# A planner that knows its side tasks' two banks: one layer of a hybrid decoder on one core

## The chip, the cores and the metric

The program runs on one core of one Trainium2 chip. The metric is device microseconds of one execution, the median of several runs. A profiled execution gives the trace that is read below.

## The reference, cut to what matters

One layer over 2048 positions of width 1024. A modulation, one projection, two groups of heads, an output projection with LayerNorm, and a SwiGLU with LayerNorm. The second head group is a recurrence over time:

```python
def rwkv7_scan(r, decay, k, v, a_vec, b_vec):
    def step(state, inp):
        r_t, w_t, k_t, v_t, a_t, b_t = inp
        sa = jnp.einsum('bhvk,bhk->bhv', state, a_t)
        state = (state * w_t[:, :, None, :] + sa[..., None] * b_t[:, :, None, :]
                 + v_t[..., None] * k_t[:, :, None, :])
        return state, jnp.einsum('bhvk,bhk->bhv', state, r_t)
...
        h = x * (1.0 + sc1) + sh1
        p = h @ w_in[l]
        mix = jnp.concatenate([short_conv_mixer(p_conv), rwkv7_mixer(p_shift)], -1) @ w_out[l]
        x = layer_norm(DEEPNORM_ALPHA * x + (1.0 + gt1) * mix, ln1_g[l], ln1_b[l])
        h = x * (1.0 + sc2) + sh2
        gate, up = jnp.split(h @ w_ffn_in[l], 2, axis=-1)
        f = (jax.nn.silu(gate) * up) @ w_ffn_out[l]
        x = layer_norm(DEEPNORM_ALPHA * x + (1.0 + gt2) * f, ln2_g[l], ln2_b[l])
```

## The kernel before, in words

**Two stages.** In the first, some 1,500 us long, the sequence is cut into four quarters of 512 positions. For each quarter TensorE runs the projection as dense products (tiles `d_...`, the output projection's `do_...`; each operand split into a high and a low part, three matmuls of 128x512 per block). The recurrence is cut into chunks of 64 positions; one quarter of one pair of heads is a *unit*, sixteen in all, written `q_hp` (0_0 to 3_3). A unit is a chain of some twenty short TensorE steps with evacuations by ScalarE, VectorE or GpSimd between them. The second stage is the SwiGLU as a fast matrix scheme (tiles `f`, then `o`).

**TensorE's order is written out by a planner.** `Interleave` holds one main stream (the dense products, `MM` = 0.216 planner-us each) and a list of side tasks (`unit`, `add`, `norm`, `mod_sums`), all Python generators. A side task yields (cost, wait[, condition]): it comes again when the planner's clock has passed the wait and the condition holds. When no side task is due, one dense matmul is put out. Only TensorE's order is fixed so; the other engines' instructions are ordered by a scheduler, except where `behind(...)` holds one behind all that its engine has been given.

**A unit's steps**, by the names that rows show: `z`, `a`, `ss`, `v`, `b` (preparation), `sn` (whose result is `Np`), `at`, `sk`, `bt`, `sr` (two banks), `x`; then the solve of the chunk's triangular system: `Np` goes out to memory and comes back as `Ns`, VectorE makes fifteen pairs of a product `pr` and a sum `G`, and `G` returns through memory in another layout (`Gd`, then eight transfers into `H16`, shown as `H`). ScalarE copies `H16` into `Gf`, VectorE transposes it to `LT`, and `pz`, `pd`, `pq`, `pg` finish the solve. Then `w` twice, `m`, `ry`, the state chain `s` (eight steps, TensorE and VectorE in turn), the output `y`, and the tail: mean and variance, `yc`, `pt` (a transpose), `yo`, `g` (the gate) and `yg`. Between the solve's last `G` and `pz` the planner leaves `D_GH` and 1.5.

**Banks.** `mm` (3) belongs to the dense products. The side tasks' steps share the tag `rb` with two banks (`RBB`); `mtt` and `ht` of `add` and `norm` are in it too. `sv` (one bank) holds `pz`, `pd`, `pq`, `pg` and also the tail's `pt` and `g`; `ch` and `y` hold the state chain and the output. A TensorE step on a bank that is still being read stops TensorE, since its order is fixed.

**The output projections** of quarters 0 to 2 are parts of the main stream (`ORDER`); that of quarter 2 stops after its first two tiles until `norm` of quarter 1 is done, and only side tasks run meanwhile.

Of the kernel before, what the change touches and what calls it, by code (L numbers as in the profile page):

```python
# [49 lines left out]
D_SS, D_B, D_SC, D_EV, D_W, D_CH, D_PT, D_G = 2.09, 7.34, 4.73, 1.5, 2.2, 1.3, 12.0, 3.34  # L50
D_ST, D_NS, D_TR, D_GH = 1.1, 13.0, 2.0, 11.0
MM = 0.216
# [18 lines left out]
class Interleave:  # L71
# [4 lines left out]
    def __init__(self):  # L76
        self.now, self.tasks = 0.0, []

# [16 lines left out]
    def __call__(self, stream, last=True):  # L95

        more = True
        while more or any(last or not t[3] for t in self.tasks):
            if self.side():
                continue  # L100
            cost = next(stream, 0) if more else None
            if cost == 0:
                more = False
            elif cost is not None:
                self.now += cost
            elif self.tasks and not self.side():
                self.now = min(t[0] for t in self.tasks if t[0] > self.now)


@with_exitstack  # L110
def kernel(
# [183 lines left out]
    def out_proj(q, spawn, raws=None):  # L295
# [12 lines left out]
        def add(n, mt):  # L308
            yield 0, 1.2
            pst = psum.tile([P, 4, P], F32, tag="rb", bufs=RBB, name=f"mtt{q}_{n}")  # L310
            for a in range(4):
                pe.transpose(pst[:, a, :], mt[:, a * P:(a + 1) * P], ident)
            xs = xz[:, :, n * P:(n + 1) * P]
            dve.scalar_tensor_tensor(out=xs, in0=xs, scalar=ALPHA, in1=pst, op0=ALU.mult, op1=ALU.add)
            yield 0.45, 0

        def norm():
            yield 0, 3.0
            for a in range(4):
                z = xz[:, a, :]  # L320
                rs = norm_stats(z, f"a{q}_{a}")
                act.activation(z, z, AF.Identity, scale=rs[:, 0:1], bias=rs[:, 1:2])
                t0 = q * QT + a * P
                load(out=xhd[t0:t0 + P, :], in_=z)
            yield 0, D_N
            hb = lnp.tile([P, KT, P], F32, tag="hb", name=f"hb{q}", bufs=1)
            for a in range(4):
                z = xz[:, a, :]
                t0 = q * QT + a * P
                for n in range(2):  # L330
                    ps = psum.tile([P, 4, P], F32, tag="rb", bufs=RBB, name=f"ht{q}_{a}_{n}")
                    for i in range(4):
                        k = 4 * n + i
                        pe.transpose(ps[:, i, :], z[:, k * P:(k + 1) * P], ident)
                    for i in range(4):
                        k = 4 * n + i
                        act.activation(hb[:, k, :], ps[:, i, :], AF.Identity, scale=s2[:, k:k + 1],
                                       bias=b2[:, k:k + 1])
                    load(out=h2d[4 * n:4 * n + 4, :, t0:t0 + P].rearrange("k p t -> p k t"),
                         in_=hb[:, 4 * n:4 * n + 4, :])  # L340
                    yield 0.45, D_H
            done.add(("norm", q))
# [15 lines left out]
    with ExitStack() as ph1:  # L358
# [63 lines left out]
        def unit(n, q, hp, r, kx, vx, lo):  # L422
# [40 lines left out]
            act.activation(sq, kx, AF.Square, scale=k_k[:, hp:hp + 1])  # L463
            yield 1.3, D_SS
            pss = psum.tile([P, NC_Q], F32, tag="rb", bufs=RBB, name="ss" + u)
# [17 lines left out]
            split(rkh, rkl, rk, dve)  # L483
            yield 0, D_B, until("y", n - 2)
            Pc = rw.tile([P, NC_Q, C + 1], F32, tag="Pc", name="Pc" + u, bufs=2)
            pool.memset(Pc[:, :, 0:1], 1.0)
# [20 lines left out]
            done.add(("prep", n))  # L507
            yield 1.5, D_SC


            first = tuple(slice(C * h, C * h + C) for h in range(2))
            ps = rb("sn")
            each(lambda c, h, hr, kr: pe.matmul(ps[hr, c, :], BK[hr, c, first[h]], Ak[hr, c, :], start=True, stop=True))
            Np = rw.tile([P, NC_Q, C], F32, tag="Np", name="Np" + u, bufs=2)
            with behind(dve):
                dve.tensor_tensor(out=Np, in0=ps, in1=rn2.unsqueeze(2).to_broadcast([P, NC_Q, C]), op=ALU.mult)
            yield 1.15, D_ST
            AV = rw.tile([P, NC_Q, 2, C], F32, tag="AV", name="AV" + u, bufs=2)
            ps1 = rb("at")
            each(lambda c, h, hr, kr: pe.matmul(ps1[hr, c, :], Ak[hr, c, :], ident[hr, hr], start=True, stop=True))  # L520
            act.copy(out=AV[:, :, 0, :], in_=ps1)
            yield 1.15, D_ST
            ps2 = rb("sk")
# [6 lines left out]
            BT = []  # L530
            for c4 in range(2):
                t = rw.tile([P, 4, 2 * C], F32, tag="BT", name=f"BT{u}_{c4}", bufs=4)
                ps3 = rb(f"bt{c4}", (4, P))
                for ci in range(4):
                    pe.transpose(ps3[:, ci, :], BK[:, 4 * c4 + ci, :], ident)
                act.copy(out=t, in_=ps3)
                BT.append(t)
                yield 0.45, D_ST

            ps4 = [rb(f"sr{h}") for h in range(2)]  # L540
            each(lambda c, h, hr, kr: pe.matmul(ps4[h][:, c, :], BK[hr, c, :], R[hr, c, :], start=True, stop=True))
# [5 lines left out]
            done.add(("bk", n))  # L547
            yield 1.8, 2 * D_ST
            ps5 = rb("x")
# [81 lines left out]
            for c4 in range(2):  # L631
                cs4 = slice(4 * c4, 4 * c4 + 4)
                ps = rb(f"w{c4}", (4, 2, C))
                for ci in range(4):
# [7 lines left out]
                yield 1.0, D_W if c4 else D_ST  # L642

            ps = rb("m")
            each(lambda c, h, hr, kr: pe.matmul(ps[hr, c, :], WT[hr, c, :], BT[c // 4][hr, c % 4, hr],
                                                start=True, stop=True))
            MT = rw.tile([P, NC_Q, C], F32, tag="MT", name="MT" + u, bufs=1)
            dve.tensor_tensor(out=MT, in0=ps, in1=id64, op=ALU.add)
            yield 1.15, D_ST
            ps1 = rb("ry")  # L650
# [11 lines left out]
            for c in range(NC_Q):  # L662
# [4 lines left out]
                if c == 0:  # L667
# [19 lines left out]
            pool.tensor_tensor(out=vs, in0=vs, in1=nhalf[:, 0:NC_Q], op=ALU.pow)  # L687
            pool.tensor_tensor(out=yc, in0=yc, in1=vs.unsqueeze(2).to_broadcast([P, NC_Q, C]), op=ALU.mult)
            yield 0, D_PT
            psT = psum.tile([P, NC_Q, C], F32, tag="sv", name="pt" + u, bufs=1)  # L690
            each(lambda c, h, hr, kr: pe.matmul(psT[hr, c, :], yc[hr, c, :], ident[hr, hr], start=True, stop=True))
            yo = t2k("yo", "yo" + u)
            act.activation(yo, psT.rearrange("p c t -> p (c t)"), AF.Identity, scale=vecs[:, V_LG + hp:V_LG + hp + 1],
                           bias=vecs[:, V_LB + hp:V_LB + hp + 1])
            pool.tensor_tensor(out=yo, in0=yo, in1=bv, op=ALU.add)
            yield 0.43, D_G
            psG = psum.tile([P, 512], F32, tag="sv", name="g" + u, bufs=1)
            pe.matmul(psG, gu[:, cols], sg, start=True, stop=True)
# [201 lines left out]
        def stream():  # L900

            for q in range(NQ):
# [8 lines left out]
                while todo:  # L911
                    at = 0
                    while todo[at][0] == "u" and not ready(NHP * q + int(todo[at][1])):
                        at = next((j for j, x in enumerate(todo) if x[0] in "co"), None)
                        if at is None:
                            yield None
                            at = 0
# [416 lines left out]
```

## Time and profile before

| | us |
|---|---|
| median of 3 runs (3058.71 to 3065.69) | 3062.82 |
| the profiled execution, its own time | 3061.64 |
| its span in the trace | 3059.8 |
| TensorE busy in the span | 2719.9 (89%) |
| VectorE, GpSimd, ScalarE busy | 1994.5, 1494.7, 1136.5 |
| mean granted clock of TensorE | 0.936 of full speed |

TensorE is busy almost throughout, so what it waits for, and at which clock it runs, is what can change. A granted clock of 1.0 is 2.4 GHz, 0.5 is 1.2 GHz; values between are means over a stretch.

### The profile page before, as it was taken

The page shows a single profiled execution, that of the slowest core. Times are in us where ns is not written, and L with a number is a line of the kernel's source. Part 1 is how long each engine was busy: PE and PEld are TensorE (multiplying, and loading weights), DVE is VectorE, ACT ScalarE, POOL GpSimd, SP SyncE. Part 2 cuts the span into 40 slices and gives each one's busy share as a digit, 9 for nine tenths or more (in the row PEclk, how much of TensorE's full clock was granted, in tenths as well). Part 3 has the DMA queues.
Part 4 walks back from the last instruction along what each step waited for, and adds up shares of the span by engine and source line. Part 5 has one row for each costly group of instructions (what it writes and reads, how often), then busy time and mean ns, then how long its engine had stood idle before and what let it go on. Part 6 is the DMA issues. An engine that isn't in the chain of part 4 may idle for free.

```text
span 3059.8 us, 50282 instructions
## 1 busy us (share of the span) xinstructions
PE 2719.9 (89%) x19232; PEld 2115.6 (69%) x19232; DVE 1994.5 (65%) x3029; ACT 1136.5 (37%) x2072; POOL 1494.7 (49%) x1171
## 2 busy tenths in 40 slices
PE   7878898889999898888779999988999988988986
PEld 5656676666777676666567888866888866766864
DVE  7445555454444645544554777798777787899698
ACT  4543433333533333333454333333333323344333
POOL 4654333323433333333544444456444467578596
PEclk8878999989999999989889999998999999999998
DMA  6442211132521221123553423223232353333333
GB/s 233 133 133 85 81 59 58 57 101 79 161 64 56 82 58 58 58 75 97 163 199 114 144 98 104 100 80 134 100 103 100 104 196 117 106 115 114 101 110 100
DMA packets 223001, 323.72 MB, mean 106 GB/s; under 512 B 55844, under 2 KB 78372, under 8 KB 222760
## 3 DMA queue, kind: packets, MB, share of 16 engines
q1 hardware_dynamic: 222760, 320.50, 33.3%
q8 instruction: 151, 2.47, 0.3%
q14 instruction: 90, 0.74, 0.1%
HBM read 244.39 MB, written 76.03 MB: 105 GB/s over the span
## 4 chain that ended last, share of the span: by engine, by line
PE 59%; DVE 18%; DMA 6%; POOL 6%; issue 4%; ACT 2%; SPq 2%; DVEq 0%; ACTq 0%; POOLq 0%
PE d L260 11%; PE f L227 9%; PE f L228 9%; PE f L226 9%; PE do L260 4%; DVE pr L575 3%; PE o L227 2%; PE o L228 2%; PE o L226 2%; DVE ws L955 2%; POOL ol L223 2%; DMA Gd<-G 2%; SPq L580 1%; DVE fl L223 1%; DMA wm<-in_wmod_dram 1%
## 5 line engine op out<-in xcount | busy, mean ns | idle before, releaser
L223 POOL TENSOR_TENSOR l<-r,h 128x512 fp32r<-128x512 f32 x201 | 266.6, 1328 | 488.3 <-ACT h L222 380.8
L226 PE MATMUL f<-uh,wh 128*128 128x512 f32 x1232 | 494.5, 401 | 10.8 <-ACT wh L222 8.1
L227 PE MATMUL f<-ul,wh 128*128 128x512 f32 x1232 | 493.0, 400 | 8.4 <-POOL ul L223 4.2
L228 PE MATMUL f<-uh,wl 128*128 128x512 f32 x1232 | 492.5, 400 | 4.7 <-POOL wl L223 4.6
L223 POOL TENSOR_TENSOR wl<-ws,wh 128x512 fp32r<-128x512 f32 x220 | 302.9, 1378 | 370.8 <-ACT wh L222 320.6
L955 DVE TENSOR_TENSOR ws<-w,w 128x512 f32<-128x512 f32 x330 | 302.7, 938 | 45.4 <-POOL ol L223 38.5
L227 PE MATMUL o<-ol,fh 128*128 128x512 f32 x616 | 252.3, 413 | 53.4 <-POOL ol L223 53.2
L974 DVE TENSOR_TENSOR c<-f,c 128x512 f32<-128x512 f32 x264 | 181.7, 688 | 159.6 <-PE f L228 95.5
L226 PEld LDWEIGHTS f<-uh,wh 128*128 128x128 f32 x1232 | 234.6, 190 | 70.8 <-ACT wh L222 10.0
L227 PEld LDWEIGHTS f<-ul,wh 128*128 128x128 f32 x1232 | 234.5, 190 | 68.4 <-POOL ul L223 6.6
L228 PEld LDWEIGHTS f<-uh,wl 128*128 128x128 f32 x1232 | 234.5, 190 | 64.5 <-POOL wl L223 7.9
L222 ACT CAST wh<-ws 128x512 fp32r<-128x512 f32 x220 | 136.7, 621 | 360.9 <-DVE ws L955 238.1
L228 PE MATMUL o<-oh,fl 128*128 128x512 f32 x616 | 246.3, 407 | 5.6 <-DVE fl L223 5.3
L226 PE MATMUL o<-oh,fh 128*128 128x512 f32 x616 | 219.8, 404 | 14.1 <-DVE c L974 6.8
L223 POOL TENSOR_TENSOR ol<-ws,oh 128x512 fp32r<-128x512 f32 x110 | 176.9, 1612 | 89.8 <-ACT oh L222 85.5
L222 ACT CAST h<-r 128x512 fp32r<-128x512 f32 x201 | 123.6, 616 | 205.3 <-PE d L260 169.5
L223 DVE TENSOR_TENSOR fl<-fr,fh 128x512 fp32r<-128x512 f32 x154 | 181.0, 1185 | 26.1 <-ACT fh L222 25.3
L227 PEld LDWEIGHTS o<-ol,fh 128*128 128x128 f32 x616 | 121.0, 196 | 96.4 <-POOL ol L223 70.8
L223 POOL TENSOR_TENSOR lo<-ro,ho 128x512 fp32r<-128x512 f32 x64 | 84.9, 1332 | 195.8 <-ACT ho L222 160.0
L226 PEld LDWEIGHTS o<-oh,fh 128*128 128x128 f32 x616 | 118.2, 193 | 45.5 <-ACT oh L222 12.4
L223 POOL TENSOR_TENSOR wl<-w,wh 128x512 fp32r<-128x512 f32 x88 | 118.6, 1348 | 60.7 <-ACT wh L222 60.7
L228 PEld LDWEIGHTS o<-oh,fl 128*128 128x128 f32 x616 | 120.4, 196 | 36.6 <-DVE fl L223 11.7
(501 smaller groups left out, 6021.9 us busy)
## 6 DMA issues: line engine op xcount, KB each, us to landing
r<-in_win_dram SPq DMA_DIRECT2D x201, 256.0 KB
w<-in_wfi_dram SPq DMA_DIRECT2D x176, 256.0 KB
fr<-fd SPq DMA_DIRECT2D x154, 256.0 KB
fd<-fs SPq DMA_DIRECT2D x110, 256.0 KB
wm<-in_wmod_dram SPq DMA_DIRECT2D x72, 256.0 KB
ro<-in_wout_dram SPq DMA_DIRECT2D x64, 256.0 KB
fd<-th SPq DMA_DIRECT2D x44, 256.0 KB
w<-in_wfo_dram SPq DMA_DIRECT2D x44, 256.0 KB
```

The costliest lines, as they stand in the source:

```text
L222: act.copy(out=hi, in_=raw)
L223: (lo_eng or pool).tensor_sub(lo, raw, hi)
L226: pe.matmul(ps, lh, rh, start=start, stop=False)
L227: pe.matmul(ps, lh, rl, start=False, stop=False)
L228: pe.matmul(ps, ll, rh, start=False, stop=stop)
L260: pe.matmul(ps, l[:, ks], r, start=kk == 0 and i == 0, stop=kk == KT - 1 and i == 2)
L575: dve.tensor_tensor(out=v, in0=G[:, :, :t + 1], in1=Nv[:, :t + 1, t].unsqueeze(1).to_broadcast([P, 8, t + 1]), op=ALU.mult)
L580: load(out=H16[16 * b:16 * b + 16, :, b % 4 * 16:b % 4 * 16 + 16], in_=Gd[b].rearrange("c j t -> j c t"))
L955: (eng or dve).tensor_tensor(out=out, in0=blocks[a], in1=blocks[b.lstrip("-")], op=ALU.subtract if b[0] == "-" else ALU.add)
L974: dve.tensor_tensor(out=c[b, t], in0=in0, in1=in1, op=op)
```

## The change

`Interleave` gets a list of the two `rb` banks, each with the planner's time at which it will be free. `run.free(n)` is a condition (n banks are free now), `run.take(n, lag)` occupies n of them until `lag` later (`D_RB` = 3.0 if none is given). Every step that uses `rb` now yields with `run.free()` first and then takes; where a step had a yield before it, the condition is joined to that, elsewhere a yield of cost 0 is added. If nothing is due, the planner's clock also jumps to the next time of a bank. Costs and waits change at `add` (1.2 to 2.0) and before `x` (1.8 and 2.2 to 2.3 and 1.1). `D_GH` goes from 11 to 15. In the tail the multiplication of `yc` and the addition to `yo` go from GpSimd to VectorE, and `pt` and `g` move from the bank `sv` to `y`. In `stream` an output projection can no longer be taken ahead of `f0`.

```diff
-D_ST, D_NS, D_TR, D_GH = 1.1, 13.0, 2.0, 11.0
+D_ST, D_NS, D_TR, D_GH = 1.1, 13.0, 2.0, 15.0
+D_RB = 3.0
...
-        self.now, self.tasks = 0.0, []
+        self.now, self.tasks, self.banks = 0.0, [], [0.0] * RBB
+
+    def free(self, n=1):
+
+        return lambda: sorted(self.banks)[n - 1] <= self.now
+
+    def take(self, n=1, lag=None):
+
+        self.banks = sorted(sorted(self.banks)[n:] + [self.now + (D_RB if lag is None else lag)] * n)
...
-                self.now = min(t[0] for t in self.tasks if t[0] > self.now)
+                self.now = min(t for t in [t[0] for t in self.tasks] + self.banks if t > self.now)
...
-            yield 0, 1.2
+            yield 0, 2.0, run.free()
+            run.take()
             pst = psum.tile([P, 4, P], F32, tag="rb", bufs=RBB, name=f"mtt{q}_{n}")
...
+                    yield 0, 0, run.free()
+                    run.take(1, D_H + 1)
                     ps = psum.tile([P, 4, P], F32, tag="rb", bufs=RBB, name=f"ht{q}_{a}_{n}")
...
-            yield 1.15, D_ST
+            yield 1.15, D_ST, run.free()
+            run.take()
             AV = rw.tile([P, NC_Q, 2, C], F32, tag="AV", name="AV" + u, bufs=2)
             ps1 = rb("at")
...
+            yield 0, 0, run.free(2)
+            run.take(2, 4.5)
             ps4 = [rb(f"sr{h}") for h in range(2)]
...
-            yield 1.8, 2 * D_ST
+            yield 2.3, D_ST, run.free()
+            run.take()
             ps5 = rb("x")
...
-            pool.tensor_tensor(out=yc, in0=yc, in1=vs.unsqueeze(2).to_broadcast([P, NC_Q, C]), op=ALU.mult)
+            dve.tensor_tensor(out=yc, in0=yc, in1=vs.unsqueeze(2).to_broadcast([P, NC_Q, C]), op=ALU.mult)
             yield 0, D_PT
-            psT = psum.tile([P, NC_Q, C], F32, tag="sv", name="pt" + u, bufs=1)
+            psT = psum.tile([P, NC_Q, C], F32, tag="y", name="pt" + u, bufs=1)
...
-            pool.tensor_tensor(out=yo, in0=yo, in1=bv, op=ALU.add)
+            dve.tensor_tensor(out=yo, in0=yo, in1=bv, op=ALU.add)
             yield 0.43, D_G
-            psG = psum.tile([P, 512], F32, tag="sv", name="g" + u, bufs=1)
+            psG = psum.tile([P, 512], F32, tag="y", name="g" + u, bufs=1)
...
-                        at = next((j for j, x in enumerate(todo) if x[0] in "co"), None)
+                        at = next((j for j, x in enumerate(todo) if x[0] in "co" and "f0" not in todo[:j]), None)
```

The same lines with `run.free()` and `run.take()` stand before `ss`, `v`, `sn`, `sk`, `bt`, `w`, `m` and `ry`.

**Three places in the built order.** TensorE where unit 3_1's `pz` comes (the names' first number is the head pair: `pz_1` is unit 3_1, `pt_0` and `g_0` the tail of 3_0, `sn_2` and `at_2` unit 3_2, `d_2` and `d_3` dense tiles of the projection). Before:

```order
L260 MATMUL d_2_12491<-h_4l,h_2_1_12512 128x512
L513 MATMUL sn_2_12521<-Ak_2_12446,BK_2_12339 64x64 x16
L691 MATMUL pt_0_12540<-kst,yc_0_12381 64x64 x16
L592 MATMUL pz_1_12560<-LT_1_12517,Np_1_11819 64x64 x16
L520 MATMUL at_2_12580<-kst,Ak_2_12446 64x64 x16
L260 MATMUL d_2_12491<-h_4h,l_2_1_12513 128x512
L260 MATMUL d_2_12491<-h_5h,h_2_1_12512 128x512
L260 MATMUL d_2_12491<-h_5l,h_2_1_12512 128x512
L599 MATMUL pd_1_12601<-H_136,Z_1_12577 64x64 x16
L698 MATMUL g_0_12624<-sg_10532,gu 128x512
L524 MATMUL sk_2_12629<-Ak_2_12446,BK_2_12339 64x64 x16
```

And in the changed kernel:

```order
L269 MATMUL d_3_12617<-h_1h,h_3_0_12620 128x512
L720 MATMUL pt_0_12628<-kst,yc_0_12473 64x64 x16
L616 MATMUL pz_1_12648<-LT_1_12605,Np_1_11836 64x64 x16
L269 MATMUL d_3_12617<-h_1l,h_3_0_12620 128x512
L269 MATMUL d_3_12617<-h_1h,l_3_0_12621 128x512
L269 MATMUL d_3_12617<-h_2h,h_3_0_12620 128x512
L269 MATMUL d_3_12617<-h_2l,h_3_0_12620 128x512
L269 MATMUL d_3_12617<-h_2h,l_3_0_12621 128x512
L530 MATMUL sn_2_12672<-Ak_2_12571,BK_2_12503 64x64 x16
L727 MATMUL g_0_12691<-sg_10239,gu 128x512
L623 MATMUL pd_1_12696<-H_136,Z_1_12665 64x64 x16
L538 MATMUL at_2_12720<-kst,Ak_2_12571 64x64 x16
```

Before, `pz_1` follows `pt_0` and `sn_2` with no dense product between; now `sn_2` comes after `pz_1`, with five dense products between them, and `g_0` precedes `pd_1`. Counted through the whole order, a unit's `sn` and its `pz` stand 131 to 174 dense products apart before and 158 to 193 now; for each unit the distance grows by 15 to 32, by 24 in the mean.

VectorE in the middle of the same unit's fifteen pairs of `pr` and `G` (`Pi`, `BK`, `rk`, `rn`, `tz`, `x` are preparation of the next unit, `S` steps of the state chain of the unit before). Before:

```order
L473 TENSOR_TENSOR Pi_2_12277<-Pi_2_12277,k_2_12186 128x512
L575 TENSOR_TENSOR pr_1_12056<-G_1_12054,Ns_1_12052 128x56
L469 TENSOR_SCALAR rn_2_12326<-ss_2_12309 128x8
L665 TENSOR_SCALAR Sst_124<-s_0_12126,Pc_0_10971 128x64
L475 TENSOR_TENSOR BK_2_12339<-Pi_2_12277,x_2_12281 128x8x64
L577 TENSOR_REDUCE G_1_12054<-pr_1_12056 128x8
L470 RECIPROCAL rn_2_12326<-rn_2_12326 128x8
L575 TENSOR_TENSOR pr_1_12056<-G_1_12054,Ns_1_12052 128x64
L480 SCALAR_TENSOR_TENSOR rk_2_12342<-rk_2_12342,vecs,r_2_12083 128x512
L577 TENSOR_REDUCE G_1_12054<-pr_1_12056 128x8
L575 TENSOR_TENSOR pr_1_12056<-G_1_12054,Ns_1_12052 128x72
```

Now:

```order
L694 TENSOR_SCALAR S_0_12221<-s_0_12223,Pc_0_10903 128x64
L599 TENSOR_TENSOR pr_1_12127<-G_1_12125,Ns_1_12123 128x64
L601 TENSOR_REDUCE G_1_12125<-pr_1_12127 128x8
L425 SCALAR_TENSOR_TENSOR k_2_12325<-d_18_12249,vecs,A 128x511
L427 SCALAR_TENSOR_TENSOR k_2_12325<-carry,vecs,A 128x1
L599 TENSOR_TENSOR pr_1_12127<-G_1_12125,Ns_1_12123 128x72
L694 TENSOR_SCALAR S_0_12221<-s_0_12223,Pc_0_10903 128x64
L601 TENSOR_REDUCE G_1_12125<-pr_1_12127 128x8
L599 TENSOR_TENSOR pr_1_12127<-G_1_12125,Ns_1_12123 128x80
L601 TENSOR_REDUCE G_1_12125<-pr_1_12127 128x8
L694 TENSOR_SCALAR S_0_12221<-s_0_12223,Pc_0_10903 128x64
```

The preparation's long instructions have left this unit's solve; between its first `pr` and its last `G` stand 22 other instructions before and 15 now. Over all sixteen units these others are 251 before and 263 now; for units 0_2 and 2_2, which now meet the start of a quarter's operands, they go from 23 to 34 and to 38.

TensorE at the stop in the output projection of quarter 2 (`do_0`, `do_1` are its first tiles, `do_2` the next, `ht` belongs to `norm` of quarter 1, `pz_3` to `g_3` to unit 3_3, `pt_2` and `g_2` to unit 3_2). The last rows of the stop before:

```order
L334 MATMUL ht_1_0_14541<-kst,xz_13755 128x128 x4
L664 MATMUL s_3_14415<-S_3_14413,MT_3_14330 64x64 x2
L671 MATMUL y_3_14439<-S_3_14413,R_3_13214 64x64 x16
L334 MATMUL ht_1_1_14582<-kst,xz_13755 128x128 x4
L334 MATMUL ht_2_0_14592<-kst,xz_13755 128x128 x4
L334 MATMUL ht_2_1_14602<-kst,xz_13755 128x128 x4
L334 MATMUL ht_3_0_14612<-kst,xz_13755 128x128 x4
L691 MATMUL pt_3_14622<-kst,yc_3_14573 64x64 x16
L334 MATMUL ht_3_1_14642<-kst,xz_13755 128x128 x4
L698 MATMUL g_3_14652<-sg_10532,gu 128x512
L260 MATMUL do_2_14663<-y_0h,ho_2_0_14666 128x512
```

The first rows of the stop now, `norm`'s first `ht` included:

```order
L346 MATMUL ht_0_0_14296<-kst,xz_13414 128x128 x4
L616 MATMUL pz_3_14306<-LT_3_14289,Np_3_13503 64x64 x16
L720 MATMUL pt_2_14325<-kst,yc_2_14171 64x64 x16
L346 MATMUL ht_0_1_14345<-kst,xz_13414 128x128 x4
L623 MATMUL pd_3_14355<-H_136,Z_3_14323 64x64 x16
L727 MATMUL g_2_14378<-sg_10239,gu 128x512
L346 MATMUL ht_1_0_14383<-kst,xz_13414 128x128 x4
L635 MATMUL pq_3_14394<-GT_3_14376,Np_3_13503 32x32 x16
L346 MATMUL ht_1_1_14413<-kst,xz_13414 128x128 x4
L645 MATMUL pg_3_14423<-Gf_133,Q_3_14393 32x32 x16
L662 MATMUL w_3_14443<-AV_3_13520,Gf_133 64x128 x8
L346 MATMUL ht_2_0_14455<-kst,xz_13414 128x128 x4
```

Before, all of unit 3_3 up to its state chain lies ahead of the stop, and its tail and six `ht` fill it. Now the stop holds all eight `ht`, unit 3_3 from `pz` to the first state step and the tail of unit 3_2, with no dense product among them.

## Rows read from the trace of the kernel before

**Rows 1.** The page: the span, and TensorE's busy time, share and instructions.

```profile
span 3059.8 us, 50282 instructions
PE 2719.9 (89%) x19232; PEld 2115.6 (69%) x19232; DVE 1994.5 (65%) x3029; ACT 1136.5 (37%) x2072; POOL 1494.7 (49%) x1171
```

**Rows 2.** Two stretches: length, busy time of each engine, granted clock, DMA share, GB/s.

```profile
130.00:1460.00 1330.00, 1168.95 (x12554) 895.12 (x12552) 668.52 (x1377) 484.17 (x916) 494.98 (x442) 0.92 0.28 82
1460.00:1475.00 15.00, 9.88 (x101) 7.02 (x100) 2.64 (x5) 11.31 (x31) 6.13 (x7) 0.77 0.55 146
```

**Rows 3.** TensorE's waits, 130 to 1620 us: total, times, longest.

```profile
PE pz L592 <- DVE LT L585: 36.1, 7, 8.3
PE pz L592 <- ACT yo L693: 26.1, 5, 8.4
PE mtt L312 <- ACT mt L353: 20.7, 10, 7.7
...
PE pt L691 <- POOL yc L688: 9.3, 6, 2.7
...
PE pz L592 <- DVE Np L516: 8.4, 1, 8.4
PE pt L691 <- POOL l L223: 7.6, 2, 4.1
...
PE sr L541 <- ACT BT L536: 7.2, 2, 4.0
PE w L636 <- DVE Ym L545: 5.4, 7, 0.9
PE w L636 <- ACT BT L536: 4.9, 1, 4.9
PE g L698 <- ACT Gf L602: 4.9, 4, 1.2
```

**Rows 4.** Timeline of unit 3_0's return: start, duration, what, idle before.

```profile
1175.21 0.29 DVE L577 TENSOR_REDUCE G<-pr 128x8 f32<-128x128 f32 x1
...
1179.23 3.81 SPq L580 DMA_DIRECT2D H<-Gd  x8
...
1184.72 0.71 DVE L585 STREAM_TRANSPOSE LT<-H 128x512 f32<-128x512 f32 x1 [4.76 <-DMA H<-Gd]
...
1185.48 1.97 PE L592 MATMUL pz<-LT,Np 64*64 64x64 f32 x32 [8.27 <-DVE LT L585]
1187.24 1.92 PE L513 MATMUL sn<-Ak,BK 64*64 64x64 f32 x32
```

**Rows 5.** The stretch around that `pz`, columns as in rows 2.

```profile
1185.00:1192.00 7.00, 6.51 (x105) 5.65 (x107) 1.12 (x2) 0.84 (x2) 0.00 (x0) 0.56 0.18 59
```

**Rows 6.** Timeline of VectorE, unit 3_1's first product and last sum.

```profile
1225.47 0.90 DVE L575 TENSOR_TENSOR pr<-G,Ns 128x16 f32<-128x16 f32 x1
...
1250.10 0.28 DVE L577 TENSOR_REDUCE G<-pr 128x8 f32<-128x128 f32 x1
```

**Rows 7.** Timeline of TensorE before and at unit 3_1's `pz`.

```profile
1248.68 1.15 PE L513 MATMUL sn<-Ak,BK 64*64 64x64 f32 x32
...
1260.06 1.97 PE L592 MATMUL pz<-LT,Np 64*64 64x64 f32 x32 [8.36 <-ACT yo L693]
```

**Rows 8.** Timeline of TensorE, two dense products with eight between.

```profile
1402.14 0.39 PE L260 MATMUL do<-y_5l,ho 128*128 128x512 f32 x1
...
1404.18 0.39 PE L260 MATMUL do<-y_0l,ho 128*128 128x512 f32 x1
```

**Rows 9.** Groups of GpSimd and VectorE by line, 130 to 1620 us.

```profile
L695 POOL TENSOR_TENSOR yo<-yo,bv 128x512 f32<-128x512 f32 x16 | 20.6, 1286 | 44.9 <-ACT yo L693 40.6 <-DMA h2d<-hb 3.3 <-PE mtt L312 1.1
L688 POOL TENSOR_TENSOR yc<-yc,vs 128x512 f32<-128x512 f32 x16 | 17.4, 1087 | 0.8
...
L475 DVE TENSOR_TENSOR BK<-Pi,x 128x512 f32<-128x512 f32 x15 | 23.4, 1561 | 0.0
...
L516 DVE TENSOR_TENSOR Np<-sn,rn 128x512 f32<-128x512 f32 x15 | 10.2, 683 | 17.3 <-PE sn L513 17.2
```

More of the change, by code (lines that the diff above doesn't have):

```diff
@@ L463, in unit @@
             act.activation(sq, kx, AF.Square, scale=k_k[:, hp:hp + 1])
-            yield 1.3, D_SS
+            run.take()
+            yield 1.3, D_SS, run.free()
+            run.take()
             pss = psum.tile([P, NC_Q], F32, tag="rb", bufs=RBB, name="ss" + u)
@@ L484, in unit @@
             yield 0, D_B, until("y", n - 2)
+            yield 0, 0, run.free()
+            run.take()
             Pc = rw.tile([P, NC_Q, C + 1], F32, tag="Pc", name="Pc" + u, bufs=2)
@@ L507, in unit @@
             done.add(("prep", n))
-            yield 1.5, D_SC
+            yield 1.5, D_SC, run.free()
             first = tuple(slice(C * h, C * h + C) for h in range(2))
+            run.take()
             ps = rb("sn")
@@ L516, in unit @@
                 dve.tensor_tensor(out=Np, in0=ps, in1=rn2.unsqueeze(2).to_broadcast([P, NC_Q, C]), op=ALU.mult)
-            yield 1.15, D_ST
+            yield 1.15, D_ST, run.free()
+            run.take()
             AV = rw.tile([P, NC_Q, 2, C], F32, tag="AV", name="AV" + u, bufs=2)
@@ L521, in unit @@
             act.copy(out=AV[:, :, 0, :], in_=ps1)
-            yield 1.15, D_ST
+            yield 1.15, D_ST, run.free()
+            run.take()
             ps2 = rb("sk")
@@ L531, in unit @@
             for c4 in range(2):
+                yield 0, 0, run.free()
+                run.take()
                 t = rw.tile([P, 4, 2 * C], F32, tag="BT", name=f"BT{u}_{c4}", bufs=4)
@@ L547, in unit @@
             done.add(("bk", n))
-            yield 1.8, 2 * D_ST
+            yield 2.3, D_ST, run.free()
+            run.take()
             ps5 = rb("x")
@@ L632, in unit @@
                 cs4 = slice(4 * c4, 4 * c4 + 4)
+                yield 0, 0, run.free()
+                run.take()
                 ps = rb(f"w{c4}", (4, 2, C))
@@ L642, in unit @@
                 yield 1.0, D_W if c4 else D_ST
+            yield 0, 0, run.free()
+            run.take()
             ps = rb("m")
@@ L648, in unit @@
             dve.tensor_tensor(out=MT, in0=ps, in1=id64, op=ALU.add)
-            yield 1.15, D_ST
+            yield 1.15, D_ST, run.free()
+            run.take()
             ps1 = rb("ry")
```

## The prediction

> **What bounds the kernel.** I read the page first: TensorE is busy for 2719.9 of 3059.8 us, so 340 us are left, and no other engine comes near [rows 1]. The table by stretches says where they lie: from 130 to 1460 us, the stage that the change touches, TensorE works for 1169 of 1330 us at a mean granted clock of 0.92, while VectorE is busy for 669 us, half of the time, and GpSimd for 495 [rows 2]. TensorE waits there for some 160 us, and the clock's missing 0.08 is, if 0.5 is the other level, 0.16 of 1330 = 213 us at half speed. The table of waits then says for what. The largest by far is `pz`, with 36.1 + 26.1 + 8.4 = 70.6 us in 13 waits; then `mtt` with 20.7, `pt` with 9.3 + 7.6 = 16.9, and single steps behind a bank [rows 3]. In the FFN stage the order does not change.
>
> The three releasers of `pz` are one cause. In the timeline of unit 3_0 the last sum `G` ends at 1175.5, the eight transfers into `H16` are issued from 1179.2, `LT` runs at 1184.7 and `pz` at 1185.5, after 8.27 us of idle TensorE [rows 4]: the return takes 10 us from `G` to `pz`. In unit 3_1 `yo` is named, because the tail shares `sv` and ScalarE sits behind the same transfers; there the first product is at 1225.5 and the last sum at 1250.1, 24.6 us, and `pz` comes 9.7 us after it [rows 6, 7]. So `pz` is late because VectorE takes 25 us for the fifteen pairs and the layout another 10, where the planner has 10 + 11 + 1.5 of its own us.
>
> **The later return, D_GH.** Four planner-us are 4 / 0.216 = 18.5 dense products. Nine of them take 1404.18 - 1402.14 = 2.04 us in the trace, 0.227 each [rows 8], so `pz` moves 4.2 us of TensorE's work later. The count through the built order, 24 dense products more between `sn` and `pz` in the mean, would be 5.4; I take 4.2, the planner's own part, since the rest is spread over bank waits. The 13 waits have a mean of 5.4 and a longest of 8.4: 13 x 4.2 = 54.6 can be filled, less about 5 for waits that were shorter than that. **-50**, with 30 (VectorE runs later too) and 70 (all of it) as bounds.
>
> What covers this: `pz` is later, but dense products fill the place, and a unit's solve has slack before the next one. Nothing behind it on TensorE is lost while the main stream has work.
>
> **VectorE in that chain.** The built order shows 22 other instructions within unit 3_1's pairs before and 15 now, but 34 and 38 against 23 in units 0_2 and 2_2, and 263 against 251 in all. An instruction over 128x512 takes 0.68 (`Np`) to 1.56 us (`BK`) [rows 9]; eleven and fifteen more at 0.7 are 8 and 10 us, of which the later `pz` covers 4.2 each: **+10** for the two (0 to +20). The units that lose instructions are already served above.
>
> **The tail on VectorE.** GpSimd takes 1.09 for `yc` and 1.29 for `yo` [rows 9], and `pt` waits 16.9 us in all for it or for the split `l` ahead of it on its queue [rows 3]. On VectorE the 32 instructions cost 0.7 to 1.6 each, 22 to 51 us on an engine that is half idle. I take half of the `pt` waits, **-8** (0 to -17), and **+5** where `yc` falls inside a solve's pairs, in about six units (0 to +10). The Trainium skill (SBUF — State Buffer, Who interferes with whom) says that a VectorE instruction with two SBUF inputs contends with a GpSimd instruction that reads SBUF, and that the later one blocks for the whole of the other. The trace agrees in kind: `BK`, two SBUF inputs, has a mean of 1561 ns, `Np`, one of them in PSUM, 683. By that rule each moved instruction could take 0.7 and a whole GpSimd instruction of 1.3, 2.0 us; the sum above goes by the rows.
>
> **pt and g in the bank y.** `g` waited 4.9 us for the copy out of `pd` in `sv` [rows 3]; with another bank this is gone: **-4** (0 to -5). In `y` they wait for reads of `y` that `yc` needs anyway, and the next unit's `y` already waits for the tail.
>
> **Two banks in the plan.** Waits on `rb` are in the rows `sr`, `w` (twice): 7.2 + 4.9 + 5.4 = 17.5 [rows 3]; `mtt` is planned 0.8 later and on a free bank. A plan with 3.0 us per bank is right only where the evacuation is prompt; where ScalarE waits for a transfer it isn't. Half of the 17.5, **-9** (0 to -17), and of `mtt` a third, since its waits are for ScalarE's copy, **-6** (0 to -12).
>
> **The clock.** Around the `pz` of unit 3_0 the granted clock is 0.56 [rows 5], and after its wait `pz` takes 1.97 and `sn` 1.92, where an undisturbed `sn` takes 1.15 [rows 4, 7]: 0.8 + 0.8, and some dense products, about 2 us a wait. If ten of 13 are gone or short: **-20** (-8 to -26). The Trainium skill (TensorE: Matmul & The Clock Gate, HAM oscillation) prices a throttled time at half its length; by that the whole stage's 213 us would hold some 106 us of penalty, an estimate that is no term of this sum.
>
> **The stop in quarter 2's output projection.** Before, it is about 15 us with 9.9 of work at a clock of 0.77 [rows 2]. Now it holds eight `ht` and unit 3_3 from `pz` to the state chain, a chain without dense products: five steps of 1.1, `w`, the small ones, each behind an evacuation. From `pz` to the first state step I come to about 20 us, near to what eight `ht` need at the pace of the six before, 15 / 6 = 2.5 each; some ten of the 20 are work that is done in any case, where before it lay between dense products. **+6** (0 to +15).
>
> **Sum.** -50 - 8 - 4 - 9 - 6 - 20 = -97; +10 + 5 + 6 = +21; together -76. From the profiled execution's 3061.6 this is 2985.6. Its own time is 1.2 below the median shown, 3062.8, so the median would be 2987. Smaller waits that are not among the rows should add some us; I forecast **2982**, 2.6% faster. All bounds at their best: 70 + 17 + 5 + 17 + 12 + 26 = 147, 2915; all at their worst: -30 - 8 + 45 = +7, 3070.
>
> **Rivals.** *The clock holds:* with nearly all waits gone TensorE scarcely falls back, and more of the 213 us comes back than ten waits at 2 us. For it: most low stretches lie at waits as in rows 5. Against: transfers into ScalarE's queue still stop `sr` and others. 2925. *The plan is filled up again:* with TensorE faster between the waits, VectorE's pairs, 25 us of steady work, come too late anew, and the bank rows show late evacuations rather than wrong places; the 4.2 us go to the pairs and the rest is eaten at the stop. Then -50 becomes about -15, -20 becomes -5, and the others cancel: 3040 to 3062. *VectorE becomes the bound:* the moved instructions and the preparation lengthen the pairs in all units as they do in 0_2 and 2_2. There 10 us more against 4.2 covered is +6; over 13 units that is +75 in place of -50 at most, and if half of the units are hit, about +35 with 5 for the clock, less 27 for the tail and the banks and with 11 for the stop and the insertions: +24, 3087. It decides once the pairs take more than about 4.2 + 3 = 7 us longer in the mean (3 is the other gains of some 40 us over 13 units). Against it: the count of instructions in the pairs hardly changes, and VectorE idles half of the stage. *The stop alone* would have to grow by 76 us to bring the time back; nothing in its rows is that long.
>
> **How the numbers follow.** The likeliest case, most of `pz` and part of the rest, 2940 to 3025: 0.62. The clock holds, below 2940: 0.13. Filled up again, 3025 to 3069: 0.12, half of it within the 0.2% (6 us) that a measurement of this kernel tells from nothing. VectorE bound, slower: 0.13. So faster 0.81, same 0.06, slower 0.13. The range reaches from 2905, near the best sum, to 3062; below it I leave 0.03 and above 0.16.
>
> **What would show it.** `pz` should fall from 70.6 us to about 20 in the waits, with 0_2 and 2_2 the longest left; the time from a last `G` to `LT` should stay near 10. `g` waiting for `Gf` and `pt` for GpSimd should vanish from the table. The granted clock from 130 to 1460 us should rise to 0.94 or more, and the stage be shorter by some 75 us while the FFN stage keeps its length. The stop should show `pz` to the state chain in 20 to 25 us. I am wrong if the pairs take well over 25 us in most units, if the state chain's `S` queues behind other VectorE work so that `s` waits, or if `pz` keeps waits of 5 us.

## The result, and the profile after

The changed kernel takes 2966.11 us (median of 4 runs, 2963.84 to 2968.76), the kernel before 3064.07 beside it: ratio 0.9684, interval 0.9667 to 0.97, or 97 us. The profiled execution took 2968.76.

The page of the changed kernel, lines as in [rows 1]:

```profile
span 2967.0 us, 50206 instructions
PE 2693.6 (91%) x19232; PEld 2093.7 (71%) x19232; DVE 2003.1 (68%) x3061; ACT 1137.3 (38%) x2072; POOL 1460.3 (49%) x1139
```

Of the 92.8 us by which the span is shorter, TensorE's busy time gives 2719.9 - 2693.6 = 26.3, for the same 19232 instructions, and its idle time the other 66.5. Where the idle time went is read from its waits, 130 to 1520 us (total, times, longest), against [rows 3]:

```profile
PE f L235 <- ACT uh L231: 20.4, 4, 7.3
PE pz L616 <- DVE LT L609: 17.9, 7, 5.8
PE s L693 <- DVE S L694: 9.9, 4, 3.9
PE d L269 <- DVE h_5l L770: 8.4, 2, 5.3
PE mtt L322 <- ACT mt L365: 7.1, 6, 3.0
PE f L236 <- DVE ul L232: 6.3, 2, 3.6
PE pt L720 <- DVE yc L717: 5.2, 3, 3.3
...
PE sr L564 <- ACT BT L557: 2.5, 2, 1.3
```

`pz` falls from 70.6 to 17.9, `mtt` from 20.7 to 7.1, `pt` from 16.9 to 5.2, `sr` from 7.2 to 2.5, and `g` is gone. Other rows have grown: `d`, where a quarter's operands are late, and at the top `f`, the first blocks of the FFN, 28.7 us in all where it was 1.2. That is work of the next stage, whose order the change does not touch.

Three stretches of the changed kernel: the first stage to 1360 us, which here takes in nearly all of the stop; from `pz` of unit 3_3 through the stop; and the FFN's entry. The columns are those of [rows 2]:

```profile
130.00:1360.00 1230.00, 1139.77 (x12465) 872.03 (x12465) 670.53 (x1400) 493.61 (x939) 465.25 (x414) 0.95 0.30 90
1336.00:1362.00 26.00, 20.40 (x317) 16.67 (x318) 7.28 (x13) 17.63 (x43) 3.05 (x4) 0.71 0.50 165
...
1400.00:1446.00 46.00, 17.41 (x64) 11.19 (x62) 35.02 (x48) 21.87 (x34) 23.09 (x21) 0.67 0.42 141
```

The granted clock is 0.95 where it was 0.92. At the FFN's entry TensorE works for 17.4 of 46 us, at 0.67. The timeline of TensorE there, first blocks `f` of the changed kernel (start, duration, idle before):

```profile
1402.47 1.02 PE L727 MATMUL g<-sg,gu 128*128 128x512 f32 x2
...
1411.80 0.49 PE L235 MATMUL f<-uh,wh 128*128 128x512 f32 x1 [0.37 <-ACT uh L231]
1414.97 0.50 PE L236 MATMUL f<-ul,wh 128*128 128x512 f32 x1 [2.68 <-DVE ul L232]
1423.50 0.79 PE L235 MATMUL f<-uh,wh 128*128 128x512 f32 x1 [7.26 <-ACT uh L231]
1425.71 0.79 PE L236 MATMUL f<-ul,wh 128*128 128x512 f32 x1 [1.42 <-POOL ul L232]
1433.50 0.80 PE L235 MATMUL f<-uh,wh 128*128 128x512 f32 x1 [6.56 <-ACT uh L231]
1437.90 0.80 PE L236 MATMUL f<-ul,wh 128*128 128x512 f32 x1 [3.61 <-DVE ul L232]
1445.38 0.79 PE L235 MATMUL f<-uh,wh 128*128 128x512 f32 x1 [6.25 <-ACT uh L231]
```

And SP's queue of the changed kernel: the last unit's store `yT`, then the loads of the FFN's operands `b`:

```profile
1404.25 0.33 SPq L730 DMA_DIRECT2D yT<-yg  x1
1404.62 23.27 SPq L1049 DMA_DIRECT2D b<-h2d  x10
1429.20 1.02 SPq L1049 DMA_DIRECT2D b<-h2d  x2
1438.64 2.69 SPq L1049 DMA_DIRECT2D b<-h2d  x2
```

The same in the kernel before, the store and then the loads, and the first `f`:

```profile
1475.86 0.33 SPq L701 DMA_DIRECT2D yT<-yg  x1
1476.30 7.94 SPq L1020 DMA_DIRECT2D b<-h2d  x3
1484.76 0.43 SPq L1020 DMA_DIRECT2D b<-h2d  x1
1495.84 1.74 SPq L1020 DMA_DIRECT2D b<-h2d  x4
1509.46 4.20 SPq L1020 DMA_DIRECT2D b<-h2d  x4
1523.27 1.65 SPq L1020 DMA_DIRECT2D b<-h2d  x2
```

```profile
1526.61 0.39 PE L226 MATMUL f<-uh,wh 128*128 128x512 f32 x1
```

In both, two of the sixteen loads are issued earlier; the other fourteen come behind the last unit's store and go on for 49 us before and 37 now. Before, the first `f` stood 1526.6 - 1475.9 = 51 us behind the store, with dense products between; now it stands 1411.8 - 1404.3 = 8 us behind it. So the first `f` comes 115 us earlier, but the last `do` of the first stage only 1642.6 - 1549.9 = 93: some 22 us are given back at the entry. From there on nothing changed: the last 1417 us hold some 1305 us of TensorE's work in both.

### The profile page after: what moved, and what is told of

Its sections match the earlier page's. It is cut to its first block, busy times and chain, and to the rows that moved or that the text cites. A ratio compares the mean times of both kernels' runs of the same rounds, so it can differ in the third digit from the quotient of the medians.

```text
span 2967.0 us, 50206 instructions
## 1 busy us (share of the span) xinstructions
PE 2693.6 (91%) x19232; PEld 2093.7 (71%) x19232; DVE 2003.1 (68%) x3061; ACT 1137.3 (38%) x2072; POOL 1460.3 (49%) x1139
## 5 line engine op out<-in xcount | busy, mean ns | idle before, releaser
L236 PEld LDWEIGHTS f<-ul,wh 128*128 128x128 f32 x1232 | 234.8, 191 | 76.2 <-DVE ul L232 12.7
L232 DVE TENSOR_TENSOR fl<-fr,fh 128x512 fp32r<-128x512 f32 x154 | 182.1, 1192 | 26.7 <-ACT fh L231 26.1
```

Of the source, the lines that this page charges most:

```text
L232: (lo_eng or pool).tensor_sub(lo, raw, hi)
L236: pe.matmul(ps, lh, rl, start=False, stop=False)
```

## The experiments

Each ratio is to the kernel before, run beside it on the same chip; a difference in us between two kernels is the difference of their ratios times 3063. An interval is about 0.0015 to either side, so such a difference is known to some 7 us. "Dense products" between two steps are counted through the built order. In the expectations A is the account of the prediction, each part worth its term, and E the theory of the entry: the FFN's first operands can be loaded and split only after the last unit's tail, and this needs a cover of dense products.

**The later return, from both sides.** In the changed kernel, and in the kernel before:

```diff
-D_ST, D_NS, D_TR, D_GH = 1.1, 13.0, 2.0, 15.0
+D_ST, D_NS, D_TR, D_GH = 1.1, 13.0, 2.0, 11.0
```

```diff
-D_ST, D_NS, D_TR, D_GH = 1.1, 13.0, 2.0, 11.0
+D_ST, D_NS, D_TR, D_GH = 1.1, 13.0, 2.0, 15.0
```

> The changed kernel with the wait for the return of the layout at 11 again, all else as changed. Theory A (the later return is the largest part): the waits of pz go from 17.9 us to 55 to 75 and the clock falls with them, 3010 to 3030 us against 2966 of the changed kernel. Theory B (the plan of the banks did it, since it moved the preparation out of VectorE's fifteen pairs, and the 4 planner-us are worth little): at most 2981 us, with the waits of pz below 30.

> The kernel before with this one number at 15. Theory A: the waits of pz fall from 70.6 us to 20 to 30, 3000 to 3020 us. Theory B: VectorE's pairs stay as long as they were and take the 4 us back, 3045 us or more. If A's and B's parts add up, this gain and that of the banks and the tail together are 98 us.

Measured: undone in the changed kernel 2974.61, ratio 0.9717 (0.9702 to 0.9731), 10 us slower than the change; alone in the kernel before 2992.41, 0.978 (0.9763 to 0.9796), 67 us faster. In the first, `pz` waits for 36.0 us, in the second for 20.2. So the part is worth 67 us by itself and 10 beside the others: its gain and theirs are largely the same waits. Of the theories, A had the waits of the second right and both times too high; B had the time of the first, but not its waits.

**The planner's banks without effect**, the condition always true, the other new costs kept:

```diff
-        return lambda: sorted(self.banks)[n - 1] <= self.now
+        return lambda: True
```

> The changed kernel with the condition on free banks always true, so that the two banks are not modelled; the new yields, the wait of 15 and the tail stay. Theory A: waits on single rb steps (sr, w, x, m) come back, 20 to 35 us, 2985 to 3005 us. Theory B: the preparation goes back into the pairs and most of the gain is lost, 3030 us or more.

Measured: 2972.49, 0.9718 (0.9701 to 0.9736), again 10 us over the change. Waits for `pz` are 28.8, for `mtt` behind `mt` 13.3, and 122 dense products now lie between the last unit's `g` and the first `f`, where the change leaves 31: the `f` waits fall to 4.3. The banks take out waits inside the stage, and part of that is handed back at the entry. Both theories had expected more. The waits of `sr` and `w` do not come back: `sr` has 3.1 us and `w` none.

**The last unit's store on ScalarE's queue**, out of the way of the loads on SP's:

```diff
-            load(out=yT[4 + hp, :, q * QT:(q + 1) * QT], in_=yg)
+            (nc.scalar.dma_start if n == NQ * NHP - 1 else load)(out=yT[4 + hp, :, q * QT:(q + 1) * QT], in_=yg)
```

> The changed kernel with the last unit's output stored from ScalarE's queue instead of SyncE's. Theory C (the FFN's first operands wait in SyncE's queue behind this store, which now comes later): the loads are issued when the weight loads ahead of them are out, some 5 us earlier, and the wait at the first FFN blocks falls from 27 to about 21 us, 2958 to 2963 us. Theory D (they wait for memory of the first stage that the last unit's tail still holds): no change, 2964 to 2969 us, and the loads still follow yg.

Measured: 2963.47, 0.9681 (0.9662 to 0.97), no change; the `f` waits are 26.7 us in place of 28.7. One load now goes 4 us ahead of the last unit's `g`. The next waits 4.0 us on the queue and is released as that `g` ends:

```profile
1394.32 1.02 PE L727 MATMUL g<-sg,gu 128*128 128x512 f32 x2
...
1395.37 1.27 SPq L1049 DMA_DIRECT2D b<-h2d  x3
```

So it is not the store's place on the queue that holds the loads. This one waits for the last unit's `g`, as theory D has it for memory that the tail still uses.

**The tail undone in the changed kernel, and alone in the kernel before.** The first puts the two instructions back on GpSimd and `pt` and `g` back into `sv`; the second does to the kernel before what the change did:

```diff
-            dve.tensor_tensor(out=yc, in0=yc, ...
+            pool.tensor_tensor(out=yc, in0=yc, ...
-            psT = psum.tile([P, NC_Q, C], F32, tag="y", name="pt" + u, bufs=1)
+            psT = psum.tile([P, NC_Q, C], F32, tag="sv", name="pt" + u, bufs=1)
-            dve.tensor_tensor(out=yo, in0=yo, in1=bv, op=ALU.add)
+            pool.tensor_tensor(out=yo, in0=yo, in1=bv, op=ALU.add)
-            psG = psum.tile([P, 512], F32, tag="y", name="g" + u, bufs=1)
+            psG = psum.tile([P, 512], F32, tag="sv", name="g" + u, bufs=1)
```

> The changed kernel with the tail as it was, pt and g in the bank sv and the two instructions on GpSimd; TensorE's order stays word for word. If the tail's move has a part of its own, waits of pt for GpSimd and of g and pg in sv come back, 10 to 20 us, 2975 to 2986 us. Rival: with the longer plan these waits are covered anyway and VectorE gets its instructions back, 2960 to 2967 us.

> The kernel before with only the tail's move; TensorE's order stays that of before. If the tail has a part of its own: the waits of pt, g and pg fall by some 20 us, 3036 to 3048 us. Rival: pz waits for its layout in any case and takes up what they leave, 3055 us or more.

Measured: undone 3000.79, 0.9799 (0.9786 to 0.9812), 35 us slower than the change, more than either theory had; alone 3061.94, 1.0006 (0.9996 to 1.0016), nothing, as the rival said. The prediction gave the tail 7 us. The next three split it.

**One half of the tail at a time.** In the changed kernel, first only the two instructions back on GpSimd (`pt` and `g` stay in `y`), then only `pt` and `g` back in `sv` (the instructions stay on VectorE); last, in the kernel before, only `pt` and `g` into `y`. The lines are those of the diff above. The expectations speak of 33 and 38 us for what the ratios put at 35 and 41.

> The changed kernel with the two tail instructions on GpSimd again and pt and g in the bank y; TensorE's order stays word for word. Undoing both halves of the tail's move cost 33 us. If GpSimd's queue is the cause (pt waits for yc behind the splits there), most of it comes back here, 2985 to 3000 us, with pt at 10 us or more of waits; if the shared bank is, 2966 to 2975 us.

> The changed kernel with pt and g in the bank sv and the two instructions on VectorE; TensorE's order stays word for word. If the shared bank is the cause of the 33 us, 2985 to 3000 us, with pd, pg and g waiting for the tail; if GpSimd's queue is, 2966 to 2975 us.

> The kernel before with one thing alone: the transpose and the product of a unit's tail write into the outputs' bank, and their element-wise instructions stay on GpSimd. TensorE's order is that of before. Undoing the bank in the changed kernel cost 38 us, while the whole tail put into the kernel before (bank and VectorE) gave nothing (ratio 1.0006), and there pz's waits rose from 70 to 100 us. If VectorE's share alone ate what the bank gave, the bank alone gives 10 to 25 us: 3036 to 3050 us, ratio 0.992 to 0.997, pz at 70 to 80. If pz takes up whatever another step stops waiting for, because its own result is late however early TensorE comes, it gives nothing: 3055 to 3065, ratio 0.998 to 1.002, with pz above 85 us.

Measured: GpSimd with `y` 2952.33, 0.9646 (0.9631 to 0.966), 12 us *faster* than the change, which neither theory had; VectorE with `sv` 3004.51, 0.9817 (0.9801 to 0.9834), 41 slower, the bank's side and beyond it; in the kernel before, `y` alone 3031.56, 0.9899 (0.9877 to 0.9921), 31 faster, above the 10 to 25 of the theory that fits. TensorE's waits of the kernel with VectorE and `sv`:

```profile
PE pz L616 <- ACT yo L722: 9.9, 5, 3.9
...
PE g L727 <- ACT Gf L626: 3.7, 3, 1.3
PE pq L635 <- DVE yg L729: 3.6, 3, 1.8
PE pt L720 <- ACT Gf L626: 3.5, 1, 3.5
...
PE pd L623 <- DVE yg L729: 3.1, 4, 0.8
```

Each of these is a step of one unit that waits for a reader of the other unit's tile in the shared bank: `pz` for `yo`, `pq` and `pd` for `yg`, `g` and `pt` for `Gf`; together 23.8 us. In the changed kernel none of these five rows is left. The bank is thus worth 31 us in the kernel before and 41 in the changed one (47 there with the instructions on GpSimd, 0.9799 against 0.9646). In the kernel before, the whole tail shows where that gain went. TensorE's waits for `pz`, first with the bank alone, then with VectorE as well:

```profile
PE pz L592 <- DVE LT L585: 67.1, 12, 7.9
```

```profile
PE pz L592 <- DVE LT L585: 99.8, 15, 13.2
```

With VectorE, the time from a unit's first `pr` to the issue of `Gd` rises to 30 us in four units (0_2 and 2_2 from 21.1, 1_1 and 3_1 from 24.9) and by 5 us in two more (1_3 and 3_3), the mean over all sixteen from 20.2 to 22.2, and `pz` waits 33 us more. The move to VectorE costs what the bank gives, 1.0006 - 0.9899, or 33 us; in the changed kernel, where `pz` comes later, it costs 12. The groups of VectorE in the changed kernel show the price of the instructions themselves, to hold against GpSimd's in [rows 9]; below each, its shortest, median and longest in ns:

```profile
L717 DVE TENSOR_TENSOR yc<-yc,vs 128x512 f32<-128x512 f32 x16 | 22.8, 1424 | 20.4 <-POOL vs L716 20.4
...
L717 DVE TENSOR_TENSOR yc<-yc,vs x16: 639/1756/1775, 272.5 to 1391.6; 128x512 f32<-128x512 f32 x16
...
L724 DVE TENSOR_TENSOR yo<-yo,bv 128x512 f32<-128x512 f32 x16 | 11.0, 688 | 16.6 <-ACT yo L722 16.6
...
L724 DVE TENSOR_TENSOR yo<-yo,bv x16: 679/692/695, 276.1 to 1399.8; 128x512 f32<-128x512 f32 x16
```

The mean of `yc` mixes two lengths: five took 0.64 to 0.69 us and eleven 1.74 to 1.78. Each of the eleven began while GpSimd ran a split (`l` or `lo`, 128x512), the five while it ran nothing. One of each kind, VectorE and then GpSimd:

```profile
901.92 1.76 DVE L717 TENSOR_TENSOR yc<-yc,vs 128x512 f32<-128x512 f32 x1 [2.07 <-POOL vs L716]
...
972.68 0.68 DVE L717 TENSOR_TENSOR yc<-yc,vs 128x512 f32<-128x512 f32 x1
```

```profile
901.86 2.95 POOL L232 TENSOR_TENSOR l<-r,h 128x512 fp32r<-128x512 f32 x2
...
975.51 2.52 POOL L232 TENSOR_TENSOR l<-r,h 128x512 fp32r<-128x512 f32 x2 [3.41 <-DMA H<-Gd]
```

`yc` waits for `vs`, which GpSimd makes, and in the eleven units GpSimd goes on to a split at the same moment; `yo` waits for ScalarE and began beside no GpSimd instruction in this kernel. No run moves `yo` alone, so how much of the 12 and 33 us these meetings cost is not shown.

**The entry of the FFN.** 15 for the first eleven units, 11 for the last five; and 13 for all:

```diff
-            yield 0, D_GH
+            yield 0, D_GH if n < 11 else 11.0
```

```diff
-            yield 0, D_GH
+            yield 0, D_GH if n < 0 else 13.0
```

> The changed kernel with the later return (15) for the first eleven units and 11 for the last five. In the built order the last unit's g then stands 145 dense products ahead of the first FFN block, as before the change, where the changed kernel has 31. Theory E (the FFN's first operands can only be made once the last unit is through, and the dense products behind it are what covers them): the wait of the first FFN blocks falls from 29 us to 6 or less, the waits of pz rise from 18 to about 25, 2943 to 2956 us. Rival F (they are held by the loads' own pace or by the norm of quarter 1): the wait stays above 20 us, 2963 to 2972 us.

> The changed kernel with the wait for the return at 13 for all units; the last unit's g stands 109 dense products ahead of the first FFN block. Theory E: the wait of the first FFN blocks is 6 us or less, those of pz 22 to 30 us, 2948 to 2960 us. Rival F: above 20 us at the FFN, 2966 to 2976 us.

Measured: by unit 2944.79, 0.962 (0.9607 to 0.9633), 20 us faster than the change; 13 for all 2967.60, 0.9693 (0.968 to 0.9707), no different. The first puts 145 dense products between the last `g` and the first `f`, as in the kernel before. Its store and loads on SP, the only `f` that waits, and the stretch that held 17.4 us of work at 0.67:

```profile
1361.67 1.34 SPq L730 DMA_DIRECT2D yT<-yg  x1
1367.91 2.22 SPq L1049 DMA_DIRECT2D b<-h2d  x4
1380.42 2.45 SPq L1049 DMA_DIRECT2D b<-h2d  x4
1393.83 3.41 SPq L1049 DMA_DIRECT2D b<-h2d  x4
1406.22 2.00 SPq L1049 DMA_DIRECT2D b<-h2d  x2
```

```profile
1412.36 0.79 PE L235 MATMUL f<-uh,wh 128*128 128x512 f32 x1 [4.98 <-ACT uh L231]
```

```profile
1400.00:1446.00 46.00, 33.43 (x143) 25.67 (x142) 37.85 (x50) 29.33 (x57) 30.56 (x26) 0.83 0.40 134
```

The loads still take 45 us from store to last group, but TensorE works meanwhile, and `pz` stays at 19.7. With 13 for all, 109 dense products lie there and the `f` waits are 5.5, as E has it, but `pz` is at 26.1, `pd` at 12.7 and `bt` at 9.0: what the entry gave, the stage took, and the time is F's.

The other runs bear E out. Wherever the last `g` stands 31 dense products ahead of the first `f` (the changed kernel and four of the runs), the `f` waits are 27 to 29 us; wherever it stands 95 or more ahead (the kernel before and eight runs), they are 1 to 6.

**Both improvements together**: the return by unit, and the tail's instructions on GpSimd with the bank `y`.

```diff
-            yield 0, D_GH
+            yield 0, D_GH if n < 11 else 11.0
...
-            dve.tensor_tensor(out=yc, in0=yc, ...
+            pool.tensor_tensor(out=yc, in0=yc, ...
-            dve.tensor_tensor(out=yo, in0=yo, in1=bv, op=ALU.add)
+            pool.tensor_tensor(out=yo, in0=yo, in1=bv, op=ALU.add)
```

> Two changes to the changed kernel at once: the return is set 15 us after the pairs for units 0 to 10 and 11 us for the last five, and the tail's two element-wise instructions are GpSimd's again, with the outputs' bank kept. Alone the first took 2966.1 to 2944.8 us (-21) and the second to 2952.3 (ratio 0.9646 against 0.9684, about -11). If the two gains lie at different places (the FFN's entry on one side, TensorE's waits for pz within the stage on the other), they add: 2930 to 2937 us, ratio 0.957 to 0.960, pz at 12 to 15 us of waiting and the FFN's first blocks under 7. If both are the same slack, seen twice, there is nothing left for the second: 2940 to 2950, ratio 0.961 to 0.963.

Measured: 2945.77, 0.9624 (0.9605 to 0.9644), the same as the return by unit alone. The gains do not add; the 12 us that VectorE cost in the changed kernel are not there once the last units return early. The kernel with the return by unit beats both kernels, by 20 and 116 us. Not tried singly are the new costs at `add` and before `x` and the rule in `stream`; they are in every run of the changed kernel.

## Why the prediction was right, step by step

**The time** was forecast at 2982 and came out at 2966; the likeliest case, "most of `pz` and part of the rest", is what happened. Undoing single parts shows that some terms were right only in their sum.

**The later return (-50).** `pz` fell by 52.7 us, to near the 20 that the prediction left it. But alone the part gave 67, and beside the rest 10, so "-50" belongs to no part. That the two do one job is seen from one common start, the kernel before with the tail as changed: with the tail alone the ratio is 1.0006, with the banks added 0.9717, with the return added (and the banks' condition off) 0.9718, with both 0.9684. The prediction added terms that share one wait. How the banks take `pz`'s waits is open: in the run with 11 they move `pz` only 5 dense products further from `sn` in the mean, and the time from first `pr` to `Gd` is 20.0 us against 22.2 with the tail alone. Two of the prediction's signs did not come. The longest wait left, 5.8 us, is in unit 2_0 and not in 0_2 or 2_2 (the only one above 5 us, which the prediction took as a sign against itself); and from the last `G` to `LT` it takes 8.5 to 18.5 us, 11.9 in the mean where it was 9.1.

**"Nothing behind it on TensorE is lost while the main stream has work"** is the step that failed. It holds inside the stage and not at its end: the last unit's `g` went from 145 to 31 dense products before the first `f`, and the entry waits for 29 us. Giving the cover back brought 20 us. One load was seen to wait for the last unit's `g` itself. Of the later ones, 9.7 us of waiting in the changed kernel are for VectorE's sums (`bh`) of operands loaded before; what holds the rest is open, except that it is not the store's place on SP's queue.

**VectorE in that chain (+10).** From first `pr` to `Gd` took 29.5 us in unit 0_2 and 30.3 in 2_2, from 21.1 in both: 8 and 9 us more, as worked out. Over all units the mean went from 20.2 to 20.9, so the rival that VectorE becomes the bound did not come in the changed kernel. The price of 10 us did not come either: `pz` waits 0 and 1.3 us in these units, where it waited 2.8 and 2.6. In the kernel before with the tail alone the pairs did lengthen, in six units.

**The tail on VectorE (-8 and +5)** had the wrong sign: +12 in the changed kernel, +33 in the kernel before. The waits of `pt` fell as said, but the price in the pairs was set for "about six units" at under 1 us each, and in the kernel before it came as 5 to 9 us in six units. The sum took VectorE's instructions at 0.7 to 1.6 us; `yc` took 1.74 to 1.78 in the eleven units where it began beside a split on GpSimd and 0.64 to 0.69 in the others. The rule that the prediction cites from the Trainium skill (SBUF — State Buffer, Who interferes with whom), by which it estimated up to 2.0 us, was the better guide: this trace agrees with it for `yc`, and `yo`, which met nothing, stayed at 0.68 to 0.70. The mean of `BK`, which the prediction read as agreement in kind, mixes two such lengths, 0.68 to 0.69 and 1.58 to 1.78.

**pt and g in the bank y (-4)** was mis-sized most: -31 to -41. It was priced by the one row that names `g`. The rows of `pz` "<- ACT yo", 26.1 us [rows 3], were put down to the late layout, and `pg` and `pd` waiting for `yg`, 4.1 and 1.0 us before, got no term. With the bank alone in the kernel before these rows vanish, yet `pz` as a whole only goes from 70.6 to 67.1; the rest of the 30 us of waits that went (195.6 to 166.0, from 130 us to the stage's last `do`) is in `mtt` (25.5 to 18.0), `pt` (17.5 to 9.3), `g` (5.8 to 0.9) and `pg` (11.5 to 6.2).

**Two banks in the plan (-9, -6).** `sr`, `w` and `mtt` lost 5.7, 8.8 and 18.4 us of waits, 33 in all, more than was said. But with the return alone in the kernel before, `w` has no waits and `sr` 1.0, and with the condition off they stay low too, so either part takes these two away; only `mtt` needs both. On the time the condition is worth 10.

**The clock (-20)** measured 26.3 us less busy time for the same instructions. It did not all come back, which leaves the rival of 2925 aside.

**The stop (+6).** Two rows of TensorE in the changed kernel mark its unit 3_3:

```profile
1338.60 1.97 PE L616 MATMUL pz<-LT,Np 64*64 64x64 f32 x32 [2.83 <-DVE LT L609]
...
1362.30 0.33 PE L693 MATMUL s<-S,MT 64*64 64x64 f32 x4
```

From `pz` to the state chain are 23.7 us, where 20 to 25 was said, with 20.4 of 26 us worked at a clock of 0.71. From the last dense product before it to the first behind it TensorE idles 8.8 us, where it was 5.1. Its net price was not measured by itself.

The errors nearly cancel, and to that extent the time came out near by luck: the bank was worth some 30 more than its term, VectorE cost 15 more, the entry took 20 to 29 that no term had, and the terms shared waits that the sum counted apart.

## What to carry to other kernels

Where one engine's order is fixed, follow a delay to the end of the stage: what hides it in the middle is gone behind the last unit, and the next stage's loads need that cover. Two chains that take turns in one bank can cost more than the rows that name the bank, 41 us for rows of 23.8 here: each step held there holds all that is queued behind it. An instruction moved to another engine may start together with the work of the engine it left; look at its shortest and longest, not at the mean. Terms that remove the same wait must not be added; undo each in the changed kernel as well as doing it alone.

## What the runs showed of the hardware

The multiplication `yc` of 128x512, both inputs in SBUF, took VectorE 0.64 to 0.69 us while GpSimd ran nothing and 1.74 to 1.78 where it began during a split of 1.27 to 1.30 us on GpSimd. The addition `yo` took 0.68 to 0.70 where it met none; in the kernel before with the tail alone three of its sixteen began during a split and took 1.53 to 1.78. On GpSimd the two took 1.09 and 1.29 [rows 9]. The granted clock at the FFN's entry was 0.67 over 46 us with 17.4 us of work, and 0.83 with 33.4; a first-stage stretch that is 93% busy had 0.95.
